# Loading a weight matrix through GpSimd with a cast, beside the first activation tiles

## The chip, the cores and the metric

The kernel runs on one core of one Trainium2 chip. The metric is the device time of one execution in microseconds, lower is better. The engines are named as in the profile: PE is the matrix engine (PEld its weight loads), DVE the vector engine, ACT the scalar engine, POOL is GpSimd, SP the sync engine, which here only issues transfers. A letter q behind a name means its instruction queue.

## The reference

A projection followed by a rotary embedding, in float32:

```python
batch, seq, hidden, n_heads = (16, 512, 768, 12)      # head_dim 64
y = np.matmul(x, weight)                              # (16, 512, 768) x (768, 768)
y = y.reshape(batch, seq, n_heads, head_dim)
y1, y2 = y[..., :32], y[..., 32:]                     # halves of each head
out1 = y1 * cos1 - y2 * sin1                          # cos, sin: (seq, head_dim), cut in halves too
out2 = y2 * cos2 + y1 * sin2
out = np.concatenate([out1, out2], axis=-1).reshape(batch, seq, hidden)
```

The input x has 25.2 MB, the output as much, the weight 2.36 MB, cos and sin 128 KB each.

## The kernel before

**Tiles.** The 8192 rows of x are worked in 32 pairs n of two tiles s = 0, 1, each tile 128 rows by 768 columns; the two tiles of a pair share the same rows of cos and sin. A tile goes through these steps:

- a load (`load`, L83, by SP) into a buffer of `xpool` (ten of them), 384 KB in rows of 3072 bytes. Some later pairs are loaded in 32-row quarters instead, by SP (`load_blocks_sp`) or by GpSimd with a cast to FP16 on the way (`load_blocks`, L99), into buffers of `bpool` (six, tag `xh`);
- a cast to FP16 (`cast`; L76 where ACT does it, L78 where DVE does), which also regroups the columns;
- six 128 x 128 transposes on the PE into one PSUM bank of `pt_pool` (L140) and a copy of that bank to SBUF, `xT` (L76 or L78 again). Pairs loaded in quarters are transposed by the DVE instead (L148);
- twelve matmuls (`mm`, L177): for each of six chunks of the weight, 128 of its rows, one matmul into each of two PSUM pieces. A pair fills three banks of `py_pool`, which has six, so two pairs are in PSUM at a time;
- the rope: for each of the three banks one DVE product with cos and sin (`rope_bank`, L187), then an addition for the pair on GpSimd (`add_pair`, L204), and a store.

**Order.** The schedule is manual: each engine executes its instructions in the order in which the program text issues them, and an engine that waits holds up all that stands behind it in its queue. The steady loop runs over n = 2 to 31; `upto` transposes and casts a few tiles ahead.

**The start**, which the change touches (L266 to L348). The DVE clears `cold`, GpSimd makes the identity (L267, L268), and the PE runs matmuls on `cold` (`warm`, L259, `WARM` = 17 in all), which also open the six PSUM banks so that later matmuls of pairs 0 and 1 only accumulate. SP issues, in this order: the four tiles of pairs 0 and 1 (L278); the weight as float32 into `w_raw`, which are buffers of `bpool` (`load_w`, L123: the first chunk in two pieces of 256 and 512 columns, then five chunks); cos and sin (L283, L284); the tiles of pairs 2 to 5 (L286); and four quarters of pair 6 (L288). The DVE casts each weight chunk into `w_sb` when it has landed (`cast_w`, L126). The matmuls of pair 0, and some of tile (1,0), follow chunk by chunk (L316 to L329); the remaining matmuls of pair 1 come after the rope of pair 0 is issued, around the transposes of tile (2,0) (L341 to L347). GpSimd's first work after the identity is `mark` (L336), a copy of one column of tile (3,0): it holds GpSimd's queue until that tile has landed, and behind it stand the casting loads of pair 8 (L337, L338) and the first addition.

CHUNKS names the six pairs (t, e) in order; "chunk 0" is CHUNKS[0] and so on.

Of the kernel before, what the change touches and what calls it, by code (L numbers as in the profile page):

```python
# [10 lines left out]
FP32 = mybir.dt.float32  # L11
# [6 lines left out]
def kernel(  # L18
# [9 lines left out]
    nc = tc.nc  # L28
    P = nc.NUM_PARTITIONS

    B, S, H = x.shape
# [7 lines left out]
    SB = S // P  # L39
    NP = B * SB // 2  # L40
    CHUNKS = [(t, e) for t in range(NT) for e in range(2)]
    AHEAD = 7
# [14 lines left out]
    cold = konst.tile([P, 512], FP16)  # L57
    sin_sb = konst.tile([P, SB, D], FP32)
    csn = konst.tile([P, 2, SB, D], FP32)
    w_sb = konst.tile([P, NT, 2, H], FP16)  # L60

    xpool = ctx.enter_context(tc.tile_pool(name="xpool", bufs=10))
    bpool = ctx.enter_context(tc.tile_pool(name="bpool", bufs=6))
# [5 lines left out]
    pt_pool = ctx.enter_context(tc.tile_pool(name="pt", bufs=2, space=bass.MemoryType.PSUM))  # L69
    py_pool = ctx.enter_context(tc.tile_pool(name="py", bufs=6, space=bass.MemoryType.PSUM))  # L70

    w_raw, xss, xhs, x16, xTT, psys, tqs, ovs = {}, {}, {}, {}, {}, {}, {}, {}

    def copy(eng, o, i_):
        if eng is nc.scalar:
            eng.copy(out=o, in_=i_)  # L76
        else:
            eng.tensor_copy(out=o, in_=i_)  # L78

    def load(n, s):  # L80
        b, r = where(n, s)
        xss[n, s] = xpool.tile([P, H], FP32, tag="xs", name="xs")
        nc.sync.dma_start(  # L83
            out=xss[n, s], in_=x[b].rearrange("(p r) h -> r p h", r=SB)[r]
        )

    def load_pair(n):
        for s in (0, 1):
            if n < NP and n not in BLOCKS and n not in BLOCKS_SP:
                load(n, s)  # L90
# [4 lines left out]
    def load_quarter(n, q, eng, dst):  # L95
        b, r = where(n, 0)
        src = x[b : b + 2].rearrange("b (j a r) (q k) -> r q a (b j) k", r=SB, a=R, q=NQ)
        dst = dst.rearrange("p s (j k) -> p (s j) k", j=NQ)
        eng.dma_start(out=dst[ts(q, R)], in_=src[r, q])  # L99
# [10 lines left out]
    def load_blocks_sp(n, q):  # L110
        if n not in BLOCKS_SP:
            return
        if q == 0:
            xhs[n] = hpool.tile([P, 2, H], FP32, tag="xf", name="xf")
            xss[n, 0], xss[n, 1] = xhs[n][:, 0], xhs[n][:, 1]
        load_quarter(n, q, nc.sync, xhs[n])

    wv = weight.rearrange("(p t e) n -> t e p n", t=NT, e=2)

    def load_w(t, e, c0=0, c1=H):  # L120
        if c0 == 0:
            w_raw[t, e] = bpool.tile([P, H], FP32, tag="xh", name="w_raw")
        nc.sync.dma_start(out=w_raw[t, e][:, c0:c1], in_=wv[t, e, :, c0:c1])  # L123

    def cast_w(t, e, c0=0, c1=H):
        nc.vector.tensor_copy(out=w_sb[:, t, e, c0:c1], in_=w_raw[t, e][:, c0:c1])  # L126

    def cast(n, s, eng):
        xc = cpool.tile([P, H], FP16, tag="xc", name="xc")
        x16[n, s] = xc  # L130
        src = xss.pop((n, s))
        src = src.rearrange("p (m t e) -> p t m e", t=NT, e=2)
        copy(eng, xc.rearrange("p (t m e) -> p t m e", t=NT, e=2), src)

    def transpose(n, s, eng):
        xc = x16.pop((n, s)).rearrange("p (t m e) -> p t e m", t=NT, e=2)
        bank = pt_pool.tile([P, 8, P], FP16, tag="pt", name="pt")
        pt = bank[:, 0 : 2 * NT].rearrange("p (t e) m -> p t e m", e=2)
        for t, e in CHUNKS:
            nc.tensor.transpose(pt[:, t, e, :], xc[:, t, e, :], ident)  # L140
        xT = tpool.tile([P, NT, 2, P], FP16, tag="xT", name="xT")
        copy(eng, xT, pt)
        xTT[n, s] = xT
# [13 lines left out]
    def psum(n, s):  # L157
        key, banks = (n, 3) if n < NP - ALONE else ((n, s), 2)
        if (n, s) == (NP - 1, 1):
            key, banks = (n, s), 3  # L160
        if key not in psys:
            psys[key] = [
                py_pool.tile([P, 512], FP32, tag="psy", name="psy") for _ in range(banks)
            ]
        ps = psys[key]
        if n >= NP - ALONE:
            cuts = (0, HH, H) if banks == 2 else (0, 5 * D, 10 * D, H)
            return [(b[:, 0 : hi - lo], lo, hi) for b, lo, hi in zip(ps, cuts, cuts[1:])]
        cut = 512 if s == 0 else 256
        return [(ps[s][:, ds(s * 256, cut)], 0, cut), (ps[s + 1][:, 0 : H - cut], cut, H)]  # L170

    def mm(n, s, t, e, c0=0, c1=H):
        for k, (ps, lo, hi) in enumerate(psum(n, s)):
            a, z = max(c0, lo), min(c1, hi)
            if a >= z:
                continue
            nc.tensor.matmul(  # L177
                ps[:, a - lo : z - lo],
                xTT[n, s][:, t, e, :],
                w_sb[:, t, e, a:z],  # L180
                start=((t, e) == CHUNKS[0] and n > 1),
                stop=((t, e) == CHUNKS[-1] and (n > 1 or s >= k)),
            )
# [65 lines left out]
        eng.dma_start(out=dst, in_=src)  # L249


    WARM = 17
    opened = [0]

    def warm(k):
        for _ in range(k):
            n, b = divmod(opened[0] % 6, 3)
            psum(n, 0)
            nc.tensor.matmul(  # L259
                psys[n][b], cold[:, 0:P], cold, start=True, stop=opened[0] < WARM - 6  # L260
            )
            opened[0] += 1

    ctx.enter_context(tc.manual_schedule())

# [3 lines left out]
        out=ident,  # L269
        in_=ident,  # L270
# [5 lines left out]
    )  # L276
    for n in (0, 1):
        load_pair(n)  # L278
    load_w(0, 0, 0, 256)
    load_w(0, 0, 256, H)  # L280
    for t, e in CHUNKS[1:]:
        load_w(t, e)
    nc.sync.dma_start(out=csn[:, 0], in_=cos.rearrange("(p r) d -> p r d", r=SB))  # L283
    nc.sync.dma_start(out=sin_sb, in_=sin.rearrange("(p r) d -> p r d", r=SB))  # L284
    for n in range(2, AHEAD - 1):
        load_pair(n)  # L286
    for q in (0, 2, 1, 3):
        load_blocks_sp(AHEAD - 1, q)  # L288


    done = {"cast": 4, "turn": 4}
# [1 line left out]
    def upto(what, k):  # L293
        while done[what] < min(k, 2 * NP):
            n, s = divmod(done[what], 2)
            done[what] += 1
            if what == "cast":
                if n not in BLOCKS:
                    cast(n, s, nc.scalar)
            elif n in BLOCKS or n in BLOCKS_SP:  # L300
                transpose_blocks(n, s)
            else:
                transpose(n, s, nc.scalar)

    warm(10)
    cast(0, 0, nc.vector)
    cast(0, 1, nc.scalar)
    transpose(0, 0, nc.vector)
    warm(2)
    transpose(0, 1, nc.scalar)  # L310
    cast(1, 0, nc.vector)
    cast(1, 1, nc.scalar)
    warm(2)
    transpose(1, 0, nc.vector)
    warm(3)
    for c0, c1 in ((0, 256), (256, H)):  # L316
        cast_w(0, 0, c0, c1)
        mm(0, 0, 0, 0, c0, c1)
        mm(0, 1, 0, 0, c0, c1)
        if c0 == 0:  # L320
            transpose(1, 1, nc.scalar)
    for k, c in enumerate(CHUNKS[1:]):
        cast_w(*c)
        if k < 2:
            mm(1, 0, *CHUNKS[k])
        mm(0, 0, *c)
        mm(0, 1, *c)
        if 1 < k < 4:
            mm(1, 0, *CHUNKS[k])  # L329

    nc.vector.tensor_copy(out=csn[:, 1, :, 0:HD], in_=sin_sb[:, :, HD:D])  # L331
    nc.vector.tensor_scalar_mul(
        out=csn[:, 1, :, HD:D], in0=sin_sb[:, :, 0:HD], scalar1=-1.0
# [4 lines left out]
    load_blocks(BLOCKS[0], (1, 3))  # L338
    rope_pair(0)
    upto("cast", 6)  # L340
    for c in CHUNKS[4:]:  # L341
        mm(1, 0, *c)
    for c in CHUNKS[:3]:
        mm(1, 1, *c)
    upto("turn", 5)
    for c in CHUNKS[3:]:
        mm(1, 1, *c)  # L347
# [2 lines left out]
    for n in range(2, NP):  # L350
# [7 lines left out]
        for s in (0, 1):  # L358
# [18 lines left out]
            for ps, lo, hi in psum(n, s):  # L377
                for c in CHUNKS:
                    mm(n, s, *c, lo, hi)
                c0, c1 = s * H + lo, s * H + hi  # L380
# [55 lines left out]
```

## Time and profile before

| | |
|---|---|
| median of six executions | 154.42 us (153.64 to 155.57) |
| the profiled execution | 153.64 us, its span from the first to the last instruction 151.8 us |
| granted PE clock, mean | 0.999 of full |
| PE / DVE / POOL / ACT busy, share of the span | 95% / 86% / 81% / 48% |
| DMA | 51.17 MB, mean 337 GB/s |
| weight cast on the DVE (L126) | 7 casts, 3.4 us |
| DMA issue on GpSimd (L99) | 20 issues, mean 593 ns |

The busy shares say which engine is used most over the whole, not which one sets the end of a stage. For that the chain of waits is read: it starts from the last instruction and goes back, at each step, to what released it. Two of the page's groups, for the reading of their columns:

```profile
L126 DVE CAST w_sb<-w_raw 128x768 f16<-128x768 f32 (+2 forms) x7 | 3.4, 500 | 2.2 <-DMA w_raw<-in_weight_dram 2.2
L99 POOL DMA_DIRECT2D xh<-in_x_dram x20 | 11.8, 593 | 0.5 <-issue 0.5
```

Line, engine, operation, what is written from what, the shapes, the count; then the total busy time in us and the mean of one in ns; then the engine's idle time just before these instructions and what ended it.

### The profile page before, as it was taken

How to read it: one execution, taken by the hardware profiler on the slowest of the kernel's cores; microseconds unless marked ns; L12 is line 12 of the kernel's file. 1: busy time of each engine (PE TensorE's matmuls, PEld its weight loads, DVE VectorE, ACT ScalarE, POOL GpSimd, SP SyncE). 2: the span in 40 equal slices, each digit the busy share in tenths (PEclk: the TensorE clock that was granted, in tenths of full speed). 3: DMA queues.
4: the chain of work that ended last, by engine and by line, in shares of the span. 5: the costliest groups of instructions: out<-in, count | busy, mean ns of one | idle time of the engine just before them, and what ended most of it. 6: DMA issues, size and time to landing. Idle time of an engine off the chain costs nothing.

```text
span 151.8 us, 2731 instructions
## 1 busy us (share of the span) xinstructions
PE 144.6 (95%) x1044; PEld 92.0 (61%) x1044; DVE 130.9 (86%) x141; ACT 73.5 (48%) x91; POOL 123.7 (81%) x69
## 2 busy tenths in 40 slices
PE   6999999999999999999999999999999999999950
PEld 2455777666656566666656566666666566666640
DVE  0667999779898989989898989999898989997890
ACT  3530696882525726282616626382617547764200
POOL 1000499999998999799997999787888879999990
PEclk9999999999999999999999999999999999999999
DMA  5999999999999999999999999999999999986554
GB/s 151 372 404 401 401 315 242 304 388 333 274 299 404 362 311 367 343 397 332 362 320 356 400 352 304 362 393 404 269 378 412 412 409 372 405 335 265 214 204 149
DMA packets 29037, 51.17 MB, mean 337 GB/s; under 512 B 7264, under 2 KB 14944, under 8 KB 29024
## 3 DMA queue, kind: packets, MB, share of 16 engines
q1 hardware_dynamic: 16640, 29.04, 55.8%
q10 hardware_dynamic: 6944, 19.99, 33.4%
q0 software_dynamic: 5440, 1.97, 11.0%
q8 instruction: 8, 0.13, 0.3%
q14 instruction: 5, 0.04, 0.1%
HBM read 27.79 MB, written 25.17 MB: 349 GB/s over the span
## 4 chain that ended last, share of the span: by engine, by line
PE 81%; POOL 7%; DMA 4%; SPq 2%; DVE 2%; POOLq 1%; issue 0%; DVEq 0%
PE psy L177 74%; PE pt L140 7%; POOL ov L204 7%; DMA w_raw<-in_weight_dram 4%; DVE tq L187 1%; SPq L123 1%; SPq L83 1%; POOLq L431 1%; DVE w_sb L126 0%; POOLq L204 0%; DVEq L187 0%
## 5 line engine op out<-in xcount | busy, mean ns | idle before, releaser
L177 PE MATMUL psy<-w_sb,xT 128*128 128x256 f16 (+3 forms) x787 | 131.5, 322 | 0.3 <-DVE w_sb L126 0.2
L187 DVE TENSOR_TENSOR tq<-psy,csn 128x1024 f32<-128x1024 f32 (+2 forms) x100 | 112.2, 1163 | 9.5 <-PE psy L177 9.1
L204 POOL TENSOR_TENSOR ov<-tq 128x1536 f32<-128x1536 f32 (+3 forms) x42 | 111.5, 2678 | 8.0 <-DVE tq L187 4.1
L177 PEld LDWEIGHTS <-xT 128*128 128x128 f16 x787 | 75.2, 98 | 45.0 <-ACT xc L76 0.5
L76 ACT COPY xT<-pt 128x768 f16<-128x768 f16 x38 | 30.3, 798 | 58.5 <-PE pt L140 54.8
L76 ACT CAST xc<-xs 128x768 f16<-128x768 f32 x38 | 33.0, 902 | 8.7 <-DMA xs<-in_x_dram 7.7
L140 PE MATMUL pt<-ident,xc 128*128 128x128 f16 x240 | 19.9, 219 | 0.3 <-DVE xc L78 0.3
L140 PEld LDWEIGHTS <-xc 128*128 128x128 f16 x240 | 16.7, 98 | 5.7 <-DVE xc L78 1.0
L336 POOL COPY mark<-xs 128x1 f32<-128x1 f32 x1 | 0.2, 183 | 15.6 <-DMA xs<-in_x_dram 15.6
L76 ACT CAST xc<-xf 128x768 f16<-128x768 f32 x14 | 12.7, 908 | 0.0
L99 POOL DMA_DIRECT2D xh<-in_x_dram x20 | 11.8, 593 | 0.5 <-issue 0.5
L148 DVE STREAM_TRANSPOSE xT<-xc 128x384 f32<-128x384 f32 x14 | 7.9, 562 | 0.0
L259 PE MATMUL psy<-cold 128*128 128x512 f16 x17 | 6.1, 506 | 1.2 <-DVE cold L266 1.2
L148 DVE STREAM_TRANSPOSE xT<-xh 128x384 f32<-128x384 f32 x10 | 7.1, 706 | 0.0
L126 DVE CAST w_sb<-w_raw 128x768 f16<-128x768 f32 (+2 forms) x7 | 3.4, 500 | 2.2 <-DMA w_raw<-in_weight_dram 2.2
L78 DVE CAST xc<-xs 128x768 f16<-128x768 f32 x2 | 1.9, 948 | 2.8 <-DMA xs<-in_x_dram 2.8
L259 PEld LDWEIGHTS <-cold 128*128 128x128 f16 x17 | 1.9, 124 | 3.5 <-issue 2.2
L78 DVE COPY xT<-pt 128x768 f16<-128x768 f16 x2 | 1.1, 558 | 1.4 <-PE pt L140 1.4
L76 ACT ACT_TABLE_LOAD x1 | 1.3, 1283 | 0.7 <-PEq L417 0.7
L266 DVE MEMSET cold<- 128x256 uint32 x1 | 0.3, 272 | 0.9 <-PEq L417 0.9
L267 POOL MEMSET ident<- 128x128 f16 x1 | 0.2, 204 | 0.3 <-POOLq L417 0.3
L331 DVE COPY csn<-sin_sb 128x128 f32<-128x128 f32 x1 | 0.2, 226 | 0.2 <-DMA sin_sb<-in_sin_dram 0.2
(9 smaller groups left out, 1.8 us busy)
## 6 DMA issues: line engine op xcount, KB each, us to landing
out_dram<-ov ACTq DMA_DIRECT2D x25, 768.0 KB, 8.4
xs<-in_x_dram SPq DMA_DIRECT2D x40, 384.0 KB, 8.8
xf<-in_x_dram SPq DMA_DIRECT2D x28, 192.0 KB, 10.4
out_dram<-ov SPq DMA_DIRECT2D x7, 384.0 KB, 2.3
out_dram<-ov SPq DMA_DIRECT2D x3, 768.0 KB, 5.5
w_raw<-in_weight_dram SPq DMA_DIRECT2D x5, 384.0 KB, 6.7
xh<-in_x_dram POOLq DMA_DIRECT2D x20, 96.0 KB, 9.6
out_dram<-ov ACTq DMA_DIRECT2D x1, 320.0 KB, 2.2
```

The lines of the kernel that those rows point to most:

```text
L76: eng.copy(out=o, in_=i_)
L78: eng.tensor_copy(out=o, in_=i_)
L83: nc.sync.dma_start(out=xss[n, s], in_=x[b].rearrange("(p r) h -> r p h", r=SB)[r])
L99: eng.dma_start(out=dst[ts(q, R)], in_=src[r, q])
L123: nc.sync.dma_start(out=w_raw[t, e][:, c0:c1], in_=wv[t, e, :, c0:c1])
L126: nc.vector.tensor_copy(out=w_sb[:, t, e, c0:c1], in_=w_raw[t, e][:, c0:c1])
L140: nc.tensor.transpose(pt[:, t, e, :], xc[:, t, e, :], ident)
L148: nc.vector.transpose(out=xT.bitcast(FP32).rearrange("p t (j a) o -> p t j (a o)", j=NQ), in_=x16.pop((n, s)).bitcast(FP32).rearrange(orde ...
L177: nc.tensor.matmul(ps[:, a - lo : z - lo], xTT[n, s][:, t, e, :], w_sb[:, t, e, a:z], start=((t, e) == CHUNKS[0] and n > 1), stop=((t, e) ...
L187: nc.vector.tensor_tensor(out=tq.rearrange("p j (h d) -> p j h d", d=D), in0=ps.rearrange("p (h d) -> p h d", d=D) .unsqueeze(1).broadcast ...
L204: eng.tensor_tensor(out=ovs[n][:, ds(c0, w)].rearrange("p (h t d) -> p h t d", t=2, d=HD), in0=tq[:, 0].rearrange("p (h t d) -> p h t d", ...
L259: nc.tensor.matmul(psys[n][b], cold[:, 0:P], cold, start=True, stop=opened[0] < WARM - 6)
```

## The change

GpSimd, instead of SP, issues the weight's six chunks, from float32 in memory straight into the FP16 tile `w_sb`; `w_raw` and `cast_w` are gone, and the first chunk is no longer cut in two. GpSimd's issues stand behind the identity and ahead of `mark`. SP issues the first four tiles and then waits: `load_others` makes the DVE copy one element of weight chunk 2 into `csn`, so that the load of cos, which overwrites it, comes after that chunk has landed; sin, the tiles of pairs 2 to 5 and the quarters of pair 6 stand behind it in SP's queue. The number of warming matmuls falls from 17 to 14, and two more (`idle`) add zeros to a bank. The matmuls of pairs 0 and 1 are put in another order: chunk 0 for pair 0 comes before the transposes of tile (1,0), tile (1,1) gets its transposes after chunk 1 and its copy by the DVE instead of ACT, and its first three chunks' matmuls are spread between those of pair 0. The rest of the kernel is as it was.

```diff
-    def load_w(t, e, c0=0, c1=H):
-        if c0 == 0:
-            w_raw[t, e] = bpool.tile([P, H], FP32, tag="xh", name="w_raw")
-        nc.sync.dma_start(out=w_raw[t, e][:, c0:c1], in_=wv[t, e, :, c0:c1])
-
-    def cast_w(t, e, c0=0, c1=H):
-        nc.vector.tensor_copy(out=w_sb[:, t, e, c0:c1], in_=w_raw[t, e][:, c0:c1])
+    def load_w(t, e):
+        nc.gpsimd.dma_start(out=w_sb[:, t, e], in_=wv[t, e])
...
-    WARM = 17
+    WARM = 14
...
+    def idle(k):
+        for _ in range(k):
+            nc.tensor.matmul(psys[1][2], cold[:, 0:P], cold, start=False, stop=False)
...
     for n in (0, 1):
         load_pair(n)
-    load_w(0, 0, 0, 256)
-    load_w(0, 0, 256, H)
-    for t, e in CHUNKS[1:]:
-        load_w(t, e)
-    nc.sync.dma_start(out=csn[:, 0], in_=cos.rearrange("(p r) d -> p r d", r=SB))
-    nc.sync.dma_start(out=sin_sb, in_=sin.rearrange("(p r) d -> p r d", r=SB))
-    for n in range(2, AHEAD - 1):
-        load_pair(n)
-    for q in (0, 2, 1, 3):
-        load_blocks_sp(AHEAD - 1, q)
+    for c in CHUNKS:
+        load_w(*c)
+
+    def load_others():
+        nc.vector.tensor_copy(
+            out=csn[0:1, 0, 0, 0:1], in_=w_sb[0:1, CHUNKS[2][0], CHUNKS[2][1], 0:1]
+        )
+        nc.sync.dma_start(out=csn[:, 0], in_=cos.rearrange("(p r) d -> p r d", r=SB))
+        nc.sync.dma_start(out=sin_sb, in_=sin.rearrange("(p r) d -> p r d", r=SB))
+        for n in range(2, AHEAD - 1):
+            load_pair(n)
+        for q in (0, 2, 1, 3):
+            load_blocks_sp(AHEAD - 1, q)
...
     transpose(0, 1, nc.scalar)
+    warm(WARM - 12)
+    mm(0, 0, *CHUNKS[0])
+    mm(0, 1, *CHUNKS[0])
     cast(1, 0, nc.vector)
     cast(1, 1, nc.scalar)
-    warm(2)
+    idle(2)
     transpose(1, 0, nc.vector)
-    warm(3)
-    for c0, c1 in ((0, 256), (256, H)):
-        cast_w(0, 0, c0, c1)
-        mm(0, 0, 0, 0, c0, c1)
-        mm(0, 1, 0, 0, c0, c1)
-        if c0 == 0:
-            transpose(1, 1, nc.scalar)
-    for k, c in enumerate(CHUNKS[1:]):
-        cast_w(*c)
-        if k < 2:
-            mm(1, 0, *CHUNKS[k])
+    for c in CHUNKS[1:2]:
         mm(0, 0, *c)
         mm(0, 1, *c)
-        if 1 < k < 4:
-            mm(1, 0, *CHUNKS[k])
+    for c in CHUNKS[:2]:
+        mm(1, 0, *c)
+    load_others()
+    transpose(1, 1, nc.vector)
+    for k, c in enumerate(CHUNKS[2:]):
+        mm(0, 0, *c)
+        mm(0, 1, *c)
+        for s, j in (((0, 2),), ((1, 0), (1, 1)), ((1, 2),), ())[k]:
+            mm(1, s, *CHUNKS[j])
...
     upto("cast", 6)
-    for c in CHUNKS[4:]:
+    for c in CHUNKS[3:]:
         mm(1, 0, *c)
-    for c in CHUNKS[:3]:
-        mm(1, 1, *c)
     upto("turn", 5)
     for c in CHUNKS[3:]:
         mm(1, 1, *c)
```

More of the change, by code (lines that the diff above doesn't have):

```diff
@@ L70 @@
     py_pool = ctx.enter_context(tc.tile_pool(name="py", bufs=6, space=bass.MemoryType.PSUM))
-    w_raw, xss, xhs, x16, xTT, psys, tqs, ovs = {}, {}, {}, {}, {}, {}, {}, {}
+    xss, xhs, x16, xTT, psys, tqs, ovs = {}, {}, {}, {}, {}, {}, {}
     def copy(eng, o, i_):
```

## The prediction

> **What bounds the kernel now.** I read the chain of work that ended last, then the waits of the first 25 us, the timeline around 15 us, and the packet records of the DMA queues (start, duration, size and queue of each packet). The chain in order of time:
>
> ```profile
> 4.49 6.71 DMA w_raw<-in_weight_dram
> 11.22 0.57 DVE w_sb L126
> 11.79 0.04 issue
> 11.84 4.42 PE psy L177 x26
> 16.26 0.34 PE pt L140 x6
> 16.59 1.78 PE psy L177 x12
> ```
>
> Columns: start, length, what. Until 11.84 us the chain is a weight chunk on its way and its cast; from there to about 134.8 us it is matmuls and transposes without a gap. So the whole of the change lies in the first 16 us, and whatever the PE gains or loses there is handed on to the end: after it the PE has no idle time in which a shift could be lost. Before 25 us the waits are:
>
> ```profile
> POOL mark L336 <- DMA xs<-in_x_dram: 15.6, 1, 15.6
> ACT xc L76 <- DMA xs<-in_x_dram: 7.7, 2, 4.9
> ...
> DVE w_sb L126 <- DMA w_raw<-in_weight_dram: 2.2, 5, 0.5
> ```
>
> (total us, times, longest). Everybody waits for transfers, little for the cast itself. Now the hand-over to pair 2, from the timeline:
>
> ```profile
> 14.93 1.87 ACT L76 CAST xc<-xs 128x768 f16<-128x768 f32 x2 [4.86 <-DMA xs<-in_x_dram]
> 15.88 0.54 PEld L140 LDWEIGHTS <-xc 128*128 128x128 f16 x6
> 16.09 0.50 PE L140 MATMUL pt<-ident,xc 128*128 128x128 f16 x6
> ```
>
> Tile x(2,0) lands at 14.93, its cast takes 0.90 and ends at 15.83; the PE reaches its transposes at 16.09. **The margin is only 0.26 us.** I call this point T20. Behind it on the PE stand the last six matmuls of tile (1,1), in both kernels, then pair 2. So T20 moving by d moves the end by d. And the DMA engines are full the whole time:
>
> ```profile
> 8.00:10.00 2.00, 1.80 (x16) 1.15 (x15) 1.36 (x4) 0.91 (x2) 0.00 (x0) 1.00 1.03 402
> 10.00:12.00 2.00, 1.85 (x11) 0.97 (x10) 1.12 (x2) 0.07 (x1) 0.00 (x0) 1.00 1.03 412
> ```
>
> The last two columns are DMA share and GB/s: saturated. So x(2,0) cannot come before the bytes in front of it: four x tiles, six weight chunks, cos, sin. In the packet records the x tiles' last packets start at 3.38, 4.32, 5.34 and 6.37, x(2,0)'s at 14.06; it is about 1.0 us for each 384 KB, made of 8 packets of 3072 bytes for each of 16 engines at 121 ns, and 0.75 to 0.87 more until the waiting engine starts.
>
> **What the Trainium skill says.** "DMA: Bandwidth & Descriptors", Queues, rings and completion order: each DMA engine takes turns between its queues, a packet at a time. The trace agrees: between 22 and 25 us, with GpSimd's and SP's loads both waiting, 535 packets of the one and 569 of the other started. Same page, Issuing engines are not separate DMA queues: a second issuing engine saves only issue time, the 16 engines are shared. So the second queue brings no bandwidth; what the trace shows at saturation is 402 to 412 GB/s. Same page, Latency and other measured facts: first byte about 1 us from GpSimd, 0.6 from SP. Here SP's first packet starts 1.0 us after its issue starts, but GpSimd's first one (issue at 17.55) at 21.86 and its next pair (33.69) at 36.60: 2.9 to 4.3 us. I use the trace. "TensorE: Matmul & The Clock Gate", Part 1: a window of some 3.4 us without work halves the clock. The trace shows full clock and no such gap.
>
> **The change, part by part.**
>
> *Removed:* seven DVE casts (0.28 + 0.42 + 5 x 0.56 = 3.5 us). The DVE idles 2.2 us between them for transfers and each overlaps the next transfer, so only one, 0.57, stood on the chain. With it gone the landing is next, and then the PE's order; I price it inside the walk below. Also removed: SP's seven weight issues (3.9 us), beside the transfers; one matmul and, net, one warming matmul, under 0.4 us in idle PE time.
>
> *Added: casting transfers.* No 3072-byte row with a cast is in the trace; the nearest is the 768-byte row of L99. In the records it takes 49 ns, where a plain 768-byte row takes 36. Filling all 16 engines' time from 22 to 25 us and subtracting the other packets at their plain price leaves 49 ns for each; beside stores (59.8 to 66.3 us) it leaves 36. So it costs 0 to 13 ns over plain. For 3072 bytes:
> - low 121 ns: the source row is as long as before and the short row shows no saving from writing half, which excludes a gain;
> - middle 134: the 13 ns are per packet. The skill's DMA page (Specifications) says that writes below 512 bytes are read first; L99's 384-byte rows would be, these 1536-byte rows not, which speaks for the lower half;
> - high 172: it is per element: 8 ns fixed (the 4-byte packets take 9) and 4 x 41.
>
> I take 134. Six chunks of 8 packets: 48 x 13 ns = **0.62 us** more DMA time before x(2,0) (0 to 2.45).
>
> *Added: GpSimd's issues.* Six at 0.58, the first 0.74 (L99), from 1.31, where the identity is built, to 4.95. GpSimd has nothing else until the mark at 16.90, so these hide; L99's issues and the adds follow the mark as before. I start the weights' packets at 3.8 (first issue's end plus the 1.75 from the last issue's end, 34.86, to 36.60), bounds 2.9 and 6.7 (the latter if all six issues must end first).
>
> *Moved: SP's other loads.* SP now stops before cos until the DVE's one-element copy, which waits for chunk 2. Behind it in SP's queue are cos, sin, eight x loads of pairs 2 to 5 and the four quarters of pair 6, and every later SP load; who waits are the rope (cos, sin), T20, and GpSimd's mark (x(3,0)). On the DVE the copy of xT(1,1) stands behind the same wait. Chunk 2 lands near 10.3, cos is issued at 10.5 and flows at 11.5. GpSimd's queue keeps the engines busy meanwhile: three chunks of 1.1 are left, 3.3 us against 1.2. So the gate wastes no DMA time; if the weight stream had run dry it would cost up to 1.2. It also does not bring x(2,0) forward: at 11.5 some 10 weight packets per engine remain, and cos, sin (16 short packets) precede x(2,0), so it still ends last, behind all the same bytes.
>
> So x(2,0) is ready for the PE at 15.83 + 0.62 = 16.45: T20 **+0.36**.
>
> *The PE's own way to T20.* Weights from 3.8 take turns with x: a pair of packets is 255 ns, so x(0,1) ends at 4.9, x(1,0) 7.0, x(1,1) 9.0, chunks 0 and 1 at 5.9 and 7.9, chunk 2 at 9.6; add 0.75 to land. x(0,1): landed 5.6, cast 6.5, transposed and copied 7.95, chunk 0's matmuls by 8.35. x(1,0): landed 7.7, cast 8.65, transposed 9.3; chunk 1 (8.7) by 9.7, tile (1,0)'s four matmuls by 10.6. x(1,1): landed 9.75, cast by 10.65, transposed by 11.05. Then 30 matmuls lead to T20 (6, 8, 6, 4 for chunks 2 to 5, and 6), at 0.17 (4.42/26 above) 5.1 us: 16.15, if chunk 5 lands by 14.35; it does, at about 14.0. That is +0.06, less than x(2,0)'s +0.36. With weights from 2.9 the x tiles are thinned out earlier, x(1,1) is a tile-time later and this way gives +1.0; with 6.7 the engines idle 0.35 and T20 is +0.7. I add 0.25 for that spread: **+0.6 us**.
>
> Downstream: the rope of pair 0 may start after its last matmul, near 15.0 instead of 14.39; the PE then has 12 matmuls and six transposes before pair 2, 2.3 us, and needs the first bank after 1.2: covered. The mark slips with x(3,0) by the same 0.6; GpSimd then has adds of 3.43 against a pair's 4.24 on the PE and absorbs it.
>
> The profiled execution took 153.64 (span 151.8, 1.8 around it), the fastest of six and 0.8 under their median, 154.42. Sum: 153.64 + 0.6 = 154.2 for it, **155.0** as a median.
>
> **The rivals.** One per cent is 1.5 us, about what a measurement of this kernel can tell.
>
> A (likeliest, 0.50): as summed, 155.0, by itself 154.1 to 155.9.
>
> B (0.28), slower: the cast is priced by the element. 172 ns make x(2,0) 2.45 later, less the margin 0.26: +2.2, 156.6. It decides beyond 1% from (1.54 + 0.26)/48 = 38 ns over plain, 159 ns a packet. For it: 49 against 36 on the short row. Against: the 36 beside stores.
>
> C (0.12), slower: GpSimd's weights start by 2.9 and starve x, +1.0, or the thinner PE work of 5 to 11 us (some 2.5 us busy) drops the clock for one window, 3.4 us of work at half speed, +1.7: 155.4 to 156.1. Against: no wait over 1.3 us in the walk.
>
> D (0.10), faster: casts cost nothing over plain, the two queues fill each other's gaps, say 410 instead of 393 GB/s over the 4.58 MB up to x(2,0), -0.5, and the PE's order gains with the DVE freed: 153.9. To pass 1% x(2,0) must land 1.3 us sooner, at 450 GB/s, which no window shows.
>
> That the loads are not truly beside the x tiles (they start at 6.7) is within A: +0.7, 155.1.
>
> **The numbers.** Slower by over 1%: most of B (0.25), two thirds of C (0.08) and A's tail (0.06): 0.39. Faster: the edge of D, with what I overlook in the start, 0.07. Within: 0.54. The range runs from D's 153.8 to past B's 156.6 with the same spread of starts, 157.3.
>
> **What would show it.** The weight packets' duration (134; 159 or more is B), their first start (3.8), x(1,1)'s cast (9.75), the cast of x(2,0) starting near 15.5, the transposes at 16.1 to 16.7, no PE idle after, and GpSimd's mark near 17.5. Wrong if a queue alone cannot fill the engines (GB/s under 380 between 9 and 11.5), or if the end moves by another amount than T20.

## The result, and the profile after

| | before | changed |
|---|---|---|
| ratio of the times | 1 | 1.0081, 95% interval 1.0059 to 1.0103 |
| in us of the median before, 154.43 | | +1.25 (+0.9 to +1.6) |
| profiled execution / its span | 153.64 / 151.8 us | 157.38 / 155.6 us |

The change makes the kernel slower by a little under one per cent. The ratio compares only the executions within 1.5% of the fastest of their kernel, which are 68 of the 72 before and 20 of the 36 changed (154.63 to 160.28 us in all); the profiled one of the changed kernel is not among them, so I read its start and not its total.

The timeline of the changed kernel, at the same place as before:

```profile
16.46 1.84 ACT L76 CAST xc<-xs 128x768 f16<-128x768 f32 x2 [6.32 <-DMA xs<-in_x_dram]
...
17.40 0.51 PE L136 MATMUL pt<-ident,xc 128*128 128x128 f16 x6 [1.22 <-ACT xc L76]
```

The cast of tile (2,0) starts at 16.46 instead of 14.93, and now the PE waits for it, 1.22 us, before the transposes at 17.40 instead of 16.09. The last entry in brackets is the idle time and what ended it. The chain of waits (start, length, what) says the same:

```profile
2.71 7.54 DMA w_sb<-in_weight_dram
...
10.27 0.15 DVE csn L285
...
11.76 5.61 DMA xs<-in_x_dram
...
17.39 0.91 ACT xc L76
18.30 0.70 ACT xT L76
...
19.05 0.83 PE psy L173 x6
```

L285 is the one-element copy that is the gate. The chain leads from the third weight chunk through the gate and SP's queue to x tiles that take 5.61 us. What carries it is no longer a weight but a tile behind the gate. The table by stretches (DMA share and GB/s are the last two columns), first of the changed kernel:

```profile
8.00:10.00 2.00, 2.00 (x16) 1.16 (x15) 0.47 (x1) 0.75 (x1) 0.00 (x0) 1.00 1.16 219
10.00:12.00 2.00, 2.00 (x17) 1.23 (x16) 0.79 (x3) 0.14 (x1) 0.00 (x0) 1.00 1.16 208
12.00:14.00 2.00, 2.00 (x14) 1.27 (x13) 0.00 (x0) 0.00 (x0) 0.00 (x0) 1.00 1.00 275
14.00:16.00 2.00, 2.00 (x14) 1.07 (x11) 0.41 (x3) 0.00 (x0) 0.00 (x0) 1.00 1.01 363
16.00:18.00 2.00, 0.78 (x10) 0.55 (x9) 2.00 (x2) 1.50 (x2) 0.00 (x0) 1.00 0.97 343
```

Then of the kernel before, from 12 us on:

```profile
12.00:14.00 2.00, 2.00 (x13) 1.16 (x12) 1.19 (x3) 0.00 (x0) 0.00 (x0) 1.00 1.05 392
14.00:16.00 2.00, 2.00 (x14) 1.26 (x13) 1.90 (x4) 1.01 (x2) 0.00 (x0) 1.00 1.04 406
16.00:18.00 2.00, 2.00 (x19) 1.24 (x17) 2.00 (x3) 1.49 (x2) 0.63 (x2) 1.00 1.03 401
```

The GB/s count what is written, and a casting transfer writes half of what it reads. Counting reads from the packet records, the changed kernel's rate is 410 and 413 KB per us in its first two rows, but 305, 363 and 343 in the last three. **The slow stretch begins where the weights end and the loads behind the gate begin.**

The DMA share stays near 1 in the slow stretch: the engines do not stand idle there, but some single packets last very long. Most packets of 3072 bytes still take 121 ns (the median), but of the 785 packets of at least 1024 bytes that SP's queue starts between 12 and 18 us, 31 last longer than 0.2 us, up to 1.7 us. In the kernel before, none of 951 does.

### The profile page after: what moved, and what is told of

Its sections match the earlier page's. It is cut to its first block, busy times and chain, and to the rows that moved or that the text cites. A ratio compares the mean times of both kernels' runs of the same rounds, so it can differ in the third digit from the quotient of the medians.

```text
span 155.6 us, 2717 instructions
## 1 busy us (share of the span) xinstructions
PE 144.5 (93%) x1042; PEld 91.6 (59%) x1042; DVE 128.3 (82%) x136; ACT 73.0 (47%) x90; POOL 126.9 (82%) x75
## 4 chain that ended last, share of the span: by engine, by line
DMA 49%; PE 33%; POOL 8%; ACT 2%; issue 1%; DVE 1%; SPq 1%; POOLq 1%; ACTq 0%; DVEq 0%
PE psy L173 30%; DMA xf<-in_x_dram 18%; DMA out_dram<-ov 16%; DMA xs<-in_x_dram 10%; POOL ov L200 7%; DMA w_sb<-in_weight_dram 5%; PE pt L136 3%; DVE tq L183 1%; ACT xc L76 1%; ACT xT L76 1%; POOL w_sb L122 1%; POOLq L434 1%; SPq L83 1%; SPq L289 0%; ACTq L245 0%
## 5 line engine op out<-in xcount | busy, mean ns | idle before, releaser
L173 PE MATMUL psy<-w_sb,xT 128*128 128x512 f16 (+3 forms) x786 | 131.4, 322 | 3.0 <-ACT xT L76 2.3
L183 DVE TENSOR_TENSOR tq<-psy,csn 128x1024 f32<-128x1024 f32 (+2 forms) x100 | 112.0, 1163 | 11.7 <-PE psy L173 11.5
L76 ACT COPY xT<-pt 128x768 f16<-128x768 f16 x37 | 29.4, 798 | 57.1 <-PE pt L136 51.3
L76 ACT CAST xc<-xs 128x768 f16<-128x768 f32 x38 | 33.0, 904 | 14.3 <-DMA xs<-in_x_dram 12.6
L255 PE MATMUL psy<-cold 128*128 128x512 f16 x14 | 5.0, 508 | 1.2 <-DVE cold L267 1.2
L78 DVE COPY xT<-pt 128x768 f16<-128x768 f16 x3 | 1.7, 558 | 3.1 <-PE pt L136 3.1
L122 POOL DMA_DIRECT2D w_sb<-in_weight_dram x6 | 3.4, 580 | 0.1
L263 PE MATMUL psy<-cold 128*128 128x512 f16 x2 | 0.6, 379 | 0.0
```

What stands on the lines that cost most here:

```text
L122: nc.gpsimd.dma_start(out=w_sb[:, t, e], in_=wv[t, e])
L173: nc.tensor.matmul(ps[:, a - lo : z - lo], xTT[n, s][:, t, e, :], w_sb[:, t, e, a:z], start=((t, e) == CHUNKS[0] and n > 1), stop=((t, e) ...
L183: nc.vector.tensor_tensor(out=tq.rearrange("p j (h d) -> p j h d", d=D), in0=ps.rearrange("p (h d) -> p h d", d=D) .unsqueeze(1).broadcast ...
L255: nc.tensor.matmul(psys[n][b], cold[:, 0:P], cold, start=True, stop=opened[0] < WARM - 6)
```

## The experiments

Two measures serve throughout. T20 is the start of the PE's transposes of tile (2,0); T21 that of tile (2,1), which also holds what the PE lost just behind T20. All times of kernels are ratios to the kernel before on the same chip.

### The changed kernel again, and tile (2,0) ahead of cos and sin

The first run is the changed kernel without an edit.

> The changed kernel once more, unedited, for a second trace of its start. Theory 1 (the end moves with the transposes of tile (2,0), and these with that tile's landing): the transposes start about 17.4 us as in the first trace, against 16.09 in the kernel before, and the time is 1.0 to 1.5 us over it. Theory 2 (the slow transfers from 12 to 18 us in the first trace, 305 to 362 KB per us, belong to that one execution): here the rate after 12 us is 390 to 410, the transposes start by 16.5, and the time is at most 0.5 us over the kernel before.

Ratio 1.0052 (1.0002 to 1.0101), some 0.8 us, less than the 1.0 to 1.5 expected. T20 is at 17.45 and the rate after 12 us is 255 and 263 KB per us: the slow stretch belongs to the change, not to one execution. But in this trace it was the PE's own order that came last: the x tiles and chunk 0 landed later (chunk 0's matmuls at 8.70, against 7.92), and the 30 matmuls up to T20 began only at 12.34.

```diff
         xss[n, s] = xpool.tile([P, H], FP32, tag="xs", name="xs")
+        if (n, s) == (2, 0):
+            nc.vector.tensor_copy(
+                out=xss[n, s][0:1, 0:1], in_=w_sb[0:1, CHUNKS[2][0], CHUNKS[2][1], 0:1]
+            )
...
     def load_others():
-        nc.vector.tensor_copy(
-            out=csn[0:1, 0, 0, 0:1], in_=w_sb[0:1, CHUNKS[2][0], CHUNKS[2][1], 0:1]
-        )
+        load(2, 0)
...
-        for n in range(2, AHEAD - 1):
+        load(2, 1)
+        for n in range(3, AHEAD - 1):
             load_pair(n)
```

> The changed kernel, with the first tile of pair 2 loaded ahead of cos and sin behind the same gate. Theory 1: the tile lands some 0.65 us earlier (256 KB at 400 KB per us), the transposes of (2,0) start near 16.7 instead of 17.4, and the time falls by 0.6 us. Rival (the end is set elsewhere, or the PE's own order sets it): the transposes start no earlier or the time stays within 0.2 us of the changed kernel.

Ratio 1.0039 (0.9982 to 1.0096), which alone doesn't tell it from the changed kernel. Its timeline does tell:

```profile
14.92 0.88 ACT L76 CAST xc<-xs 128x768 f16<-128x768 f32 x1 [3.97 <-DMA xs<-in_x_dram]
...
16.78 0.50 PE L140 MATMUL pt<-ident,xc 128*128 128x128 f16 x6
...
17.38 0.89 ACT L76 CAST xc<-xs 128x768 f16<-128x768 f32 x1 [1.58 <-DMA xs<-in_x_dram]
18.17 0.80 ACT L76 COPY xT<-pt 128x768 f16<-128x768 f16 x1
...
19.02 0.83 PE L177 MATMUL psy<-w_sb,xT 128*128 128x256 f16 x6 [0.77 <-ACT xT L76]
```

Tile (2,0) starts its cast 1.5 us sooner, as in the kernel before, and T20 comes at 16.78, now set by the PE's own order. But tile (2,1) is still late, at 17.38. Its cast stands in ACT's queue ahead of the copy of xT(2,0), so that copy ends late and the PE waits 0.77 us for it. The gain at T20 is gone by T21 (19.69, against 19.72). Not one tile is late but all that stands behind the gate.

### The gate taken away, and the gate alone

```diff
     def load_others():
-        nc.vector.tensor_copy(
-            out=csn[0:1, 0, 0, 0:1], in_=w_sb[0:1, CHUNKS[2][0], CHUNKS[2][1], 0:1]
-        )
```

> The changed kernel without the gate: SP issues cos, sin and the later tiles straight behind its first four. Theory 3 (the gate, by restarting SP's queue, delays tile (2,0)): it lands before 14 us, but the weights share the engines with it and the later tiles, the last chunk lands after 15.5, and the PE loses there: time 1 us or more above the changed kernel. If the gate costs more than it gives, the time is below the changed kernel by 0.5 us or more.

```profile
13.90 0.88 ACT L76 CAST xc<-xs 128x768 f16<-128x768 f32 x1 [3.75 <-DMA xs<-in_x_dram]
14.34 1.14 PE L173 MATMUL psy<-w_sb,xT 128*128 128x512 f16 x6 [0.54 <-DMA w_sb<-in_weight_dram]
...
16.27 1.78 PE L173 MATMUL psy<-w_sb,xT 128*128 128x512 f16 x10 [0.80 <-DMA w_sb<-in_weight_dram]
```

Ratio 1.0092 (1.0053 to 1.0130). Tile (2,0) lands before 14 us and there is no slow stretch (401 to 418 KB per us from 12 us on). But the weights share the engines with tiles that nobody needs yet, and the PE waits for them, 1.3 us in all. So without the gate the changed kernel loses about as much, by another path; the further 1 us that I expected did not come.

Next, the gate alone in the kernel before: weights as float32 by SP, with DVE casts and the old order. The one-element copy, from `w_raw` of chunk 2, and behind it the loads of cos, sin and the later tiles stand after the cast of chunk 2.

```diff
+    def load_others():
+        nc.vector.tensor_copy(
+            out=csn[0:1, 0, 0, 0:1], in_=w_raw[CHUNKS[2]][0:1, 0:1]
+        )
+        nc.sync.dma_start(out=csn[:, 0], in_=cos.rearrange("(p r) d -> p r d", r=SB))
...
         cast_w(*c)
+        if k == 1:
+            load_others()
```

> The kernel before, with the gate alone: cos, sin and the later tiles wait for the third weight chunk, whose loads are all issued already. Prediction's view (the gate wastes no transfer time while chunks remain): tile (2,0) lands at 14.9 to 15.0 and the time is that of the kernel before within 0.2 us. Rival (restarting SP's queue opens a hole or slows what follows): tile (2,0) lands 1 us later or more, near 16, and the time rises by 0.8 us or more.

The timeline, then the table by stretches:

```profile
13.66 0.56 DVE L126 CAST w_sb<-w_raw 128x768 f16<-128x768 f32 x1 [0.41 <-DMA w_raw<-in_weight_dram]
...
16.59 1.86 ACT L76 CAST xc<-xs 128x768 f16<-128x768 f32 x2 [6.28 <-DMA xs<-in_x_dram]
...
17.53 0.51 PE L140 MATMUL pt<-ident,xc 128*128 128x128 f16 x6 [0.81 <-ACT xc L76]
```

```profile
12.00:14.00 2.00, 1.82 (x12) 1.01 (x11) 1.19 (x3) 0.00 (x0) 0.00 (x0) 1.00 0.87 256
14.00:16.00 2.00, 2.00 (x14) 1.23 (x13) 1.70 (x4) 0.00 (x0) 0.00 (x0) 1.00 1.03 301
16.00:18.00 2.00, 1.19 (x13) 0.67 (x12) 2.00 (x3) 1.33 (x2) 0.00 (x0) 1.00 0.90 290
```

Ratio 1.0070 (1.0033 to 1.0106). From the last chunk's cast to tile (2,0)'s it is 2.93 us, against 1.72 in the kernel before. **The gate alone, with no load on GpSimd and no casting transfer, costs nearly as much as the whole change**, with a slow stretch and a wait at T20 of the same kind (70 of SP's 722 packets between 12 and 18 us last longer than 0.2 us). That is the rival's forecast.

### The gate's place

> The kernel before with the same gate set on the first weight chunk instead of the third: SP stops and starts again, but some 2.5 us sooner, with about 3.5 us of weight transfers still ahead of what it issues. Theory 4 (what follows a gate is slow only while SP has not yet issued far ahead of the transfers): no slow stretch, tile (2,0)'s cast starts at 15.2 or earlier, the transposes of (2,0) by 16.3, and the time is within 0.3% of the kernel before. Rival (every stop of SP's queue slows its next loads, wherever it is): the rate falls to about 300 KB per us again, tile (2,0) lands after 16, and the time is 0.7% up as with the later gate.

```profile
12.00:14.00 2.00, 1.84 (x12) 0.98 (x11) 1.12 (x2) 0.00 (x0) 0.00 (x0) 1.00 1.05 387
14.00:16.00 2.00, 2.00 (x14) 1.21 (x13) 1.59 (x4) 0.04 (x1) 0.00 (x0) 1.00 1.04 403
```

The edit is the one above with `CHUNKS[0]`, called after the cast of that chunk's first piece. SP starts again at 8.94 us instead of 11.37, and the slow stretch is gone. The ratio is 1.0013 (0.9988 to 1.0038). The absolute times of the expectation were missed (cast at 15.96, T20 at 17.02), since in this trace the weights also came 0.9 us late, before the gate mattered; from the last chunk's cast to tile (2,0)'s it is 1.83 us, close to the 1.72 without a gate.

In the changed kernel a first edit names the earlier chunk and leaves the copy in its place:

```diff
-            out=csn[0:1, 0, 0, 0:1], in_=w_sb[0:1, CHUNKS[2][0], CHUNKS[2][1], 0:1]
+            out=csn[0:1, 0, 0, 0:1], in_=w_sb[0:1, CHUNKS[0][0], CHUNKS[0][1], 0:1]
```

> The changed kernel with the gate on the first weight chunk instead of the third. Theory 4: tile (2,0) lands near 14 and there is no slow stretch, but the weights now share the engines with it from about 9.5 us: the last chunk lands after 14.8 and the PE waits for weights, so the time is within 0.3% of the changed kernel, with the wait moved from the tile to the weights. Rival (the gate's place is all that is wrong): the time falls to that of the kernel before.

The copy waited for an earlier chunk, but it stood on the DVE behind the copy of xT(1,0) and ran at 10.12 us, where the changed kernel's ran at 10.27. SP's restart hardly moved, the slow stretch stayed (317 and 340 KB per us), and its six times scatter from 154.70 to 159.59 us, too widely for a ratio. It says nothing of an earlier gate. The next edit moves the copy as well:

```diff
     cast(1, 0, nc.vector)
+    load_others()
     cast(1, 1, nc.scalar)
...
-    load_others()
     transpose(1, 1, nc.vector)
```

> The changed kernel with the gate on the first weight chunk and, unlike the try before, moved up on the DVE to just behind tile (1,0)'s cast, so that SP starts again near 8.5 us instead of 10.4. Theory 4 (a gate costs where SP has no lead when the weights run out): no slow stretch after 12 us (380 KB per us or more), cos, sin and tile (2,0) share the engines with the last chunks, both land near 14.8, the transposes of (2,0) start near 16.4, and the time is 0.5% or more below the changed kernel, within 0.4% of the kernel before. Rival (with two queues the weights come too late whatever the gate, as without it): the PE waits for the last chunks by 0.5 us or more and the time stays 0.7% or more above the kernel before.

```profile
8.16 0.13 DVE L285 CAST csn<-w_sb 1x1 f32<-1x1 f16 x1
8.32 0.33 SPq L288 DMA_DIRECT2D csn<-in_cos_dram  x1
...
15.33 1.87 ACT L76 CAST xc<-xs 128x768 f16<-128x768 f32 x2 [5.07 <-DMA xs<-in_x_dram]
...
16.29 0.51 PE L136 MATMUL pt<-ident,xc 128*128 128x128 f16 x6
```

```profile
12.00:14.00 2.00, 2.00 (x14) 1.19 (x13) 0.15 (x1) 0.00 (x0) 0.00 (x0) 1.00 1.08 370
14.00:16.00 2.00, 2.00 (x15) 1.23 (x13) 1.31 (x3) 0.67 (x1) 0.00 (x0) 1.00 1.03 415
```

Ratio 0.9989 (0.9960 to 1.0017): with the gate two microseconds earlier, and nothing else edited, the change costs nothing that can be measured. T20 is at 16.29, as expected.

> The same early gate, with tile (2,0) ahead of cos and sin. Theory 4: tile (2,0) lands 0.6 us or more sooner than with the early gate alone, near 14, but the PE's own order reaches its transposes only at 16.2 to 16.5, so the time is that of the early gate within 0.3%. If tile (2,0) still sets the end there, it falls by another 0.4%.

Ratio 1.0003 (0.9969 to 1.0036). Tile (2,0)'s cast starts at 13.88 and T20 is at 15.82, 0.27 us earlier than in the kernel before; the span is 151.7 us. Neither version beats the kernel before by more than can be measured.

From the packet records, ordered by what SP had issued behind its gate when the first packet of these loads moved. The last column counts the packets of at least 1024 bytes in SP's queue that start between 12 and 18 us and last longer than 0.2 us:

| kernel | SP issues again | first packet | issues by then | KB per us, 12 to 14 / 14 to 16 us | long packets |
|---|---|---|---|---|---|
| changed, again | 11.61 | 12.57 | 2 | 255 / 263 | 56 |
| tile (2,0) first | 11.16 | 12.14 | 3 | 251 / 296 | 66 |
| float32 by GpSimd (next section) | 10.83 | 11.95 | 3 | 236 / 298 | 50 |
| before, gate on chunk 2 | 11.37 | 12.38 | 3 | 256 / 301 | 70 |
| changed | 10.44 | 11.92 | 4 | 305 / 363 | 31 |
| chunk 0, copy not moved | 10.28 | 12.01 | 4 | 317 / 340 | 39 |
| before, gate on chunk 0 | 8.94 | 12.39 | 6 | 387 / 403 | 0 |
| early gate | 8.32 | 11.80 | 8 | 403 / 415 | 0 |
| early gate, tile (2,0) first | 7.84 | 11.36 | 8 | 395 / 415 | 0 |

The kernel before and the changed kernel without the gate have no long packets there either. What the long ones last beyond the usual 46 ns (1024 bytes) or 121 ns (3072 bytes), added up and shared among the 16 engines, is 0.7 to 1.3 us in the six slow rows: an estimate, of the order of the loss.

So the place of the gate decides. Wherever SP restarts, the packets behind the gate move only at 11.4 to 12.6 us, when the last weight chunk is on its way, and with at most four transfers issued by then the next 4 us are slow. The number issued, the time since the restart and the moment of the restart go together in these rows, so they do not show which of them counts. What inside the DMA engines makes single packets long after a short lead is not settled.

### The cast in the transfer

GpSimd loads the chunks as float32 into `w_raw` and the DVE casts them. The gate stays on chunk 2 (its copy now reads `w_raw`), and so does the order, but for the cast of tile (1,0), which goes ahead of chunk 0's on the DVE.

```diff
-        nc.gpsimd.dma_start(out=w_sb[:, t, e], in_=wv[t, e])
+        nc.gpsimd.dma_start(out=w_raw[t, e], in_=wv[t, e])
...
+        nc.vector.tensor_copy(out=w_sb[:, t, e], in_=w_raw[t, e])
```

> The changed kernel without the cast in the transfer: GpSimd loads the weight chunks as float32 and the DVE casts them, six casts of 0.56 us; gate and order as in the changed kernel, but tile (1,0)'s cast goes ahead of the first chunk's on the DVE. Prediction's term (the cast costs 13 ns a packet, 0.1 us a chunk): the chunks that have the engines to themselves come 0.1 us closer together than in the changed kernel. Rival (the cast costs no transfer time): they come at the same 0.95 us, the wait for tile (2,0) stays as it is, and the time is the changed kernel's or up to 0.6 us above it, for the first chunk's cast on the way of the PE.

Chunks 3 and 4, which have the engines to themselves, take 0.967 and 0.969 us from first to last packet as float32, and 0.946 each with the cast. GpSimd's float32 load moves in packets of 6144 bytes, so the two are not alike packet by packet; but SP's plain loads of 3072-byte rows in the kernel before moved 412 KB per us between 10 and 12 us, and the casting chunks 413. The cast costs no transfer time. The ratio is 1.0146 (1.0106 to 1.0185), and it is the DVE:

```profile
13.12 1.95 DVE L128 CAST w_sb<-w_raw 128x768 f16<-128x768 f32 x4
13.72 5.03 PE L179 MATMUL psy<-w_sb,xT 128*128 128x512 f16 x30 [1.11 <-DVE w_sb L128]
```

The casts of chunks 2 to 5 stand behind the copy of xT(1,1), which ends at 13.20, so the PE waits 1.11 us and reaches T20 only at 18.59. That was more than the 0.6 us I allowed for. In this order the casting transfer is worth some 0.65% against loading as float32; the casts must go somewhere, and here they stood in the way.

### The whole, and what is left

If the end moves with the start, each span must differ from 151.8 by what T21 differs from 18.21, plus any PE wait later on:

| kernel | T21 | shift | PE waits after 22 us | sum | span less 151.8 |
|---|---|---|---|---|---|
| no gate | 19.95 | 1.74 | 0 | 1.7 | 1.7 |
| before, gate on chunk 2 | 19.87 | 1.66 | 0 | 1.7 | 1.9 |
| before, gate on chunk 0 | 19.17 | 0.96 | 0.45 | 1.4 | 1.6 |
| float32 by GpSimd | 20.64 | 2.43 | 0 | 2.4 | 2.4 |
| early gate | 18.62 | 0.41 | 0 | 0.4 | 0.4 |
| early gate, tile (2,0) first | 18.08 | -0.13 | 0 | -0.1 | -0.1 |
| changed | 19.72 | 1.51 | 2.11 | 3.6 | 3.8 |
| tile (2,0) first | 19.69 | 1.48 | 0.83 | 2.3 | 2.5 |
| chunk 0, copy not moved | 18.89 | 0.68 | 2.04 | 2.7 | 2.9 |

The start explains the spans within 0.2 us, apart from one wait near 93 us in some traces. In the changed kernel's timeline it is this:

```profile
93.37 0.38 ACTq L245 DMA_DIRECT2D out_dram<-ov  x1
93.85 1.50 ACT L76 COPY xT<-pt 128x768 f16<-128x768 f16 x2 [5.81 <-DMA xf<-in_x_dram]
...
94.70 3.53 PE L173 MATMUL psy<-w_sb,xT 128*128 128x512 f16 x21 [2.11 <-ACT xT L76]
```

A store in ACT's queue is issued 0.08 us after the landing of an `xf` load that had used the same completion semaphore, and the copies behind the store come late. The kernel before has such stores too, without a PE wait. The wait is in all four traces that have a late gate and casting loads, and, shorter (0.45), in the kernel before with the gate on chunk 0, but not in the other two with a late gate. Why is open, and in the repeated run of the changed kernel 1.9 us of its 5.8 us of longer span are left over after T21 (+1.81) and this wait (2.11).

## Why the prediction was right or wrong

**The forecast** (no change beyond 1%, 155.0 us, +0.6) has the right sign, and the measured +1.25 us, about twice the +0.6, lies inside the range and under 1%. But the sum reached it through the wrong term: +0.62 us for the cast, which costs nothing, stood where a loss of about 1.1 us at the gate belonged, which was put at nothing. That the two are of like size is luck.

**What bounds the kernel: right in kind, but T20 is not the point.** The table of spans shows for nine kernels that the end moves with the PE's start, but by the shift of T21. With tile (2,0) first, T20 moved by 0.69 and T21 by 1.48; with the early gate by 0.20 and 0.41. That "the end moves by another amount than T20" was named as a sign of being wrong, and it came true: I had counted six matmuls behind T20 and overlooked ACT, where the cast of tile (2,1) and the copy of xT(2,0) stand one behind the other. The forecast of "no PE idle after" failed too, by the 2.11 us near 93 us. The engines were full with GpSimd's loads alone, as expected (413 KB per us between 10 and 12 us), and the PE's own way was right: the matmuls before T20 end at 16.18 in the changed kernel's trace, predicted 16.15. That way varies by more than the 0.25 us I added, though: in the repeated run it reached T20 at 17.45.

**The cast's price: right by the packet, wrong in the sum.** The packet lasts 134 to 135 ns, the predicted middle. I multiplied 13 ns by 48 packets to +0.62 us. But packets overlap: the DMA share is 1.16 while the casting chunks have the engines alone, and a chunk takes 0.946 us, less than the 0.967 of float32. The term measures zero, and with it rival B falls. A duration that is longer is a cost only if nothing runs beside it; the share above 1 in the kernel before was the hint.

**The gate: the step that failed.** "So the gate wastes no DMA time", I wrote, since three chunks were left, 3.3 us against a restart of 1.2 us. Cos was issued at 10.44 us, predicted 10.5, but the count was wrong: by the time that a chunk has landed, the next is nearly through, and two chunks were left (15.4 packets per engine), not three. SP's first packet moved at 11.92, predicted 11.5, with 3.1 weight packets per engine to go instead of some 10. Even so the engines did not run dry: the share stays near 1. What I left out is what follows: single packets last up to 1.7 us, the rate falls to 305 and 363 KB per us, and the cast of tile (2,0), predicted near 15.5, starts at 16.46. I priced a restart at "up to 1.2 if the weight stream had run dry", and at nothing otherwise. The gate alone measures +0.70% (0.33 to 1.06), 1.1 us, with the weights not yet run dry when it opened. I had the price nearly right, and the condition for it wrong.

**Taking turns: right at first, wrong at the restart.** The Trainium skill ("DMA: Bandwidth & Descriptors", Queues, rings and completion order) has each engine take turns between its queues. While x and weights were both under way they did: tile (1,1) and chunk 1 end together (8.62 and 8.47 us; predicted 9.0 and 7.9). But with the early gate SP issued at 8.32 and had no packet moving until 11.80, while GpSimd's ran at 140 to 153 packets per us. The measurement decides: a queue that restarted beside a full one moved nothing for 3.5 us here. Whether it was passed over or its transfers had not yet reached the engines is not shown.

**The others.** GpSimd's first weight packet came at 5.05 us, in the bounds of 2.9 to 6.7 and later than the 3.8 taken. Rival C's early start did not occur; where the x tiles came late all the same, in the repeated run, what delayed them is not known. The mark moved from 16.90 to 18.39, by T21's amount and not by 0.6. The clock did not drop in the first 20 us. Rival D's gain at T20 appears with the early gate and tile (2,0) first: 0.27 us, too little to show in the time.

## What to carry to other kernels

A wait that holds back a queue's loads is not free because other transfers fill the engines meanwhile: ask how far ahead the queue will have issued by the time that it must carry the load alone, and open the gate early enough (here 2 us earlier took the whole loss away). A DMA share near 1 does not show that the transfers run at full rate: look at the bytes moved, and at the longest packets. A gate made by a copy on a busy engine opens when that engine reaches the copy, not when its data are there. And price a transfer by the time from first to last packet of a stream that has the engines alone, not by the duration of a packet.

## What the hardware showed that I had not expected

- Behind a restart of SP's queue with 2 to 4 transfers issued when the first packet moved, the DMA engines moved 236 to 363 KB per us between 12 and 16 us; with 6 or 8 issued, 387 to 415.
- The loss sits in few packets: 31 to 70 of some 650 to 810 in SP's queue lasted 0.2 to 1.9 us in the slow traces, while the DMA share of no stretch of 2 us fell below 0.87; the median stayed at 121 ns for 3072 bytes.
- Beside GpSimd's full stream SP's restarted queue had its first packet 3.5 us after its first issue (8.32 to 11.80, and 7.84 to 11.36), with later restarts 1.0 to 1.7 us after it, and 1.0 us at the start of the kernel, when nothing else ran.
- A transfer that casts float32 rows of 3072 bytes to FP16 is as fast as one that doesn't (0.946 us for 384 KB read, against 0.967), although each packet lasts 134 ns and not 121.
